# Joining small TensorE products into fewer visits in a hybrid mLSTM and attention decoder step

## The chip, the cores and the metric

The kernel runs on one core of a Trainium2 chip. The metric is the device time of one execution in microseconds; lower is better. The engines are called as in the profile: PE (TensorE, matrix products), DVE (VectorE), ACT (ScalarE), POOL (GpSimd), SP (SyncE, which issues most DMAs).

## What is computed

One layer of a decoder is applied to a prompt of 1024 tokens and to 8 samples of 4 tokens each (32 rows), with a width of 1024. Two branches run in parallel: an mLSTM with 4 heads of 128, in chunks of 128 tokens for the prompt, and sliding-window attention with 8 heads and 2 key-value heads. Both are gated and added back to the input. Cut to what matters here:

```python
h, gate = adaln_in(x, c, w_ada, b_ada, g_norm)
(mq, mk, mv, mi, mf, mo, mz, aq, ak, av, az, gm, ga) = split_in(h @ w_in)
y_m, C, n, m = mlstm_branch(mq, mk, mv, mi, mf, mo, mz, C0, n0, m0, b_i, b_f, g_mn)
...                                       # y_a: window attention, gated by silu(az)
u = sigmoid(gm) * (y_m @ w_mo) + sigmoid(ga) * (y_a @ w_ao)
x = x + gate * (u @ w_o)

# mlstm_chunk, per head: the samples' chunk has 4 tokens and starts from a given state C, n, m
num = einsum('bhts,bhse->bhte', s, v) + w_inter[..., None] * einsum('bhtd,bhde->bhte', q, C)
dot = sum(s, -1) + w_inter * einsum('bhtd,bhd->bht', q, n)
h = num / maximum(abs(dot), exp(-m_hat))[..., None]
...
# mlstm_branch, behind all chunks
h = h * rsqrt(mean(h * h, -1, keepdims=True) + NORM_EPS)
h = h * g_mn * sigmoid(mo) * silu(mz)
```

## The kernel before

All weights and activations are float32. A large product is made of three products in float32r (high part by high, high by low, low by high), 128 weights wide, with 288 to 512 columns; these are called long products here. From about a quarter of the time on they come in pairs of weight columns (`block_products`, class `Pair`): seven block products numbered 1 to 7 stand for eight, on 512 tokens at a time, into the banks `bx`, `bw`, `by` and `bz`. There are 18 such pairs: 4 of the mLSTM's inputs (`head_in`), 8 of gates (`gate`), 2 of `query_gate` and 4 of `head_gate`. Four further pairs for the attention's output (`AttPair`, `att_products`, banks `ax` to `az`) follow, then plain products by `w_mo` and by `w_o`.

Everything else on PE is small float32 products put between the long ones. PE's order is written out by the program: `mm` and `tr` append each product behind the last one (`in_order`). Class `Side` decides where small work goes. It holds generators in streams (`m` the prompt's heads, `a` the attention units, `s` the samples, `x` and `g` preparations). After each triple of long products `side.tick()` looks for generators that are due. Its clock `side.now` is a sum of estimated product times. A generator yields a lag and the PSUM banks its next step needs (`a`, `b`, `o`); a step that needs banks goes only at a visit, which comes at the earliest 1.5 us of that clock after the last one, and each bank is held back for a while after it was used (`HOLD`). Every tag of PSUM has two buffers, taken in turn.

The small products that the change touches, by the names that the profile shows:

- `smp`: the 32 sample rows against the raw weights of a pair, sixteen products of 32 columns each, spread over four column groups of the array (`Pair.samples`); its sum is copied to `smps`.
- `smpo`: one product that adds the four parts of `smps` (`samples_end`); its result goes to the pair's kind (`kind.samples`). In `block_products` it stands behind block product 6, while the next pair's `smp` stands behind product 2 (product 7 for the first pair).
- `ty`: transposition of the prompt head's eight normalised blocks (`head`, `stage_d`), three visits of 3, 3 and 2, each a step after the scaling of its blocks on DVE (`stage_c3`).
- `stk`, `sS`, `sn`, `sU`, `st`, `sty`: the steps of a sample head (`sample_head`), one of four: transposed keys and values, scores, numerator, state update (`sU`, two visits of 2 and 1), the sum over four partition groups (`st`), and the transposition of the normalised result (`sty`). Between `st` and `sty` stand a square sum on ACT and a chain of small DVE operations (`factors`) on 32 rows.
- `pt`, `oT`, `sc`: attention units; `tk`, `tv`, `S`, `U`, `n`: steps of the prompt's heads; they are not changed but lie beside the others.

On-chip memory: most tiles come from the tag `half` (128 x 512 float32), 49 buffers taken in turn. An unused tile `lead` of 56 values stands near the front of the allocation.

Of the kernel before, what the change touches and what calls it, by code (L numbers as in the profile page):

```python
# [37 lines left out]
C_END = 849  # L38
LEAD = 56

# [73 lines left out]
class Side:  # L114
# [25 lines left out]

    def tick(self):
        self.each()
        for st in self.streams.values():
            if st["wait"] and len(st["live"]) < st["max"] and self.now >= st["next"]:
                self.begin(st)
        used, visit = set(), self.now >= self.last + self.quiet
        for item in sorted((i for st in self.streams.values() for i in st["live"]), key=lambda i: i[1]):
            banks = set(item[2])
            if self.now < item[1] or used & banks or (banks and not visit) or any(self.now < self.free.get(b, 0) for b in banks):
                continue  # L150
            used |= banks
# [23 lines left out]
def body(tc, a):  # L175
    nc = tc.nc
    with ExitStack() as ctx:
# [17 lines left out]
        def ht(shape, name, dt=F32):  # L195
            return sp.tile(shape, dt, tag="half", bufs=49, name=name)

# [110 lines left out]
        load_x(1, 0, KT, xT[1])  # L308
        cp.tile([128, LEAD], F32, name="lead")
        cst = cp.tile([128, C_END], F32, name="cst")  # L310
# [287 lines left out]
        def gates(gp, zg, bias):  # L598
            gate_sums(gp, zg, (8,))
            ig = cp.tile([128, 36], F32, name="ig")  # L600
            x = cp.tile([128, 36], F32, name="fx")
            for t, o in ((ig, 0), (x, 4)):
# [4 lines left out]
                V.tensor_tensor(t[:NS, 32:36], gp[:NS, 8, o:o + 4], bias[:NS, o:o + 4], op=ALU.add)  # L607
            e = cp.tile([128, 36], F32, name="fe")
            S.activation(e, x, AF.Abs)
            S.activation(e, e, AF.Exp, scale=-1.0)  # L610
            r = cp.tile([128, 36], F32, name="fr")
            q = cp.tile([128, 36], F32, name="fq")
            lf = cp.tile([128, 36], F32, name="lf")
# [25 lines left out]
            gt4 = ht([32, 4, 128], "gt4")  # L639
            gt2 = ht([32, 2, 128], "gt2")  # L640
            aT, bT, zero, cm = (gt4[:, i] for i in range(4))
            nm, wi = gt2[:, 0], gt2[:, 1]
            aTs = cp.tile([NH, NS], F32, name="aTs")
# [387 lines left out]
        def head(h):  # L1031
# [100 lines left out]
            def stage_d(p):  # L1132
                cs = GROUPS[p]
                m = len(cs)
                c0, w = cs[0] * 128, m * 128
                ns = w_.pop(p)
                ty = pb([128, 3, 128], f"ty{h}_{p}")
                for i in range(m):
                    tr(ty[:, i], ns[:, i, 0:128], ident)
                y = ht([128, 384], "yt")[:, :w]  # L1140
                S.activation(y, ty[:, :m].rearrange("p c e -> p (c e)"), AF.Copy, scale=gmn[:, h:h + 1])
                issue(yhD[h][:, c0:c0 + w], y, eng=nc.gpsimd)

            for visit in ([(load, 0), 11.0, ""], [(prep, 0), 3.0, "ob"], [(stage_e, 0), (stage_a, 0), 7.0, "o"],
# [3 lines left out]
                          [(stage_e, 2), (stage_c, 1), (stage_a, 2), 7.0, "o"], [(stage_b, 2), 5.0, "o"],  # L1148
                          [(stage_c, 2), 5.0, ""], [(stage_f, 0), 4.0, ""], [(stage_c3, 0), 4.0, "b"],
                          [(stage_d, 0), (stage_c3, 1), 4.0, "b"], [(stage_d, 1), (stage_c3, 2), 4.0, "b"], [(stage_d, 2), 0.0, ""]):  # L1150
                for fn, p in visit[:-2]:
# [5 lines left out]
            if h == 2:  # L1157
                at["n0"], at["n1"] = (cp.tile([128, NH, NB], F32, name=n) for n in ("n0", "n1"))
                dma(at["n0"], a["state_n"])
                for i in range(NH):  # L1160
                    side.add("s", sample_head(i), "ob")

        def sample_head(h):
# [53 lines left out]
            for c, b, m in zip(Cs, bs, ns_):  # L1217
                V.tensor_tensor(c[:, :m], c[:, :m], sxb[:, h, 2, b].unsqueeze(2).to_broadcast((128, m, 129)), op=ALU.mult)
            yield 4.0, "b"
            for i, (c, b, m) in enumerate(zip(Cs, bs, ns_)):  # L1220
                up = pb([128, 388], f"sU{h}_{i}")
                mm(up[:, :m * 129 + m % 2], kn, vms[i][1][:, :m * 129 + m % 2], start=True, stop=True)
                V.tensor_tensor(c[:, :m], c[:, :m], up[:, :m * 129].rearrange("p (b e) -> p b e", e=129), op=ALU.add)
                store(a["C_s"][h][:, b], c[:, :m, 0:128])
                G.tensor_copy(at["n1"][:, h, b], c[:, :m, 128])
                if i == 1:
                    yield 1.5, "b"
            yield 3.0, "o"
            tot = po([128, 129], f"st{h}")
            mm(tot[:NS], cst[:, C_S32:C_S32 + NS], ns4, start=True, stop=True)  # L1230
            ns = sm([NS, 129], "sns", 1)
            S.copy(ns, tot[:NS])
            ssq = sm([NS, 1], "sssq", 2)
            jk = sm([128, 128], "mjk", 2, BF16)
            S.activation(jk[:NS], ns[:, 0:128], AF.Square, accum_out=ssq)
            yield 2.5, ""
            den = sm([NS, 1], "fsden", 2)
            size(den, ns[:, 128:129])
            d, r = factors(den, fls[:, h:h + 1], ssq, [NS, 1], "fs")
            yield 4.0, ""  # L1240
            V.tensor_scalar(ns[:, 0:128], ns[:, 0:128], d, r, op0=ALU.mult, op1=ALU.mult)
            yield 4.0, "b"
            ty = pb([128, NS], f"sty{h}")
            tr(ty, ns[:, 0:128], ident[:NS, :NS])
            V.tensor_scalar(gs[:, h], ty, gmn[:, h:h + 1], None, op0=ALU.mult)
            samples_done.append(h)
            if h == NH - 1:
# [247 lines left out]
        def block_products(jobs, hook):  # L1495
# [178 lines left out]
        def att_products():  # L1674
# [26 lines left out]
            for j, (n, i) in enumerate(flat):  # L1701
# [647 lines left out]
```

## Time and profile before

| | |
|---|---|
| time, median of 3 runs | 835.4 us (835.07 to 835.62) |
| the profiled execution's own time | 835.73 us |
| its span from first to last instruction | 833.9 us |
| PE busy | 813.9 us (98%) |
| DVE busy | 597.2 us (72%) |
| ACT busy | 421.7 us (51%) |
| granted TensorE clock | 0.999 |
| bytes moved | 153.95 MB, mean 185 GB/s |

How to read it: busy time is the union of an engine's instructions. PE's rows overlap, since a product starts while the one before it drains, so the cost of a product is seen in the distance between starts, not in its duration. A row of the timeline has the start and the duration in us, the engine, the line, the operation, the tile written and the tiles read, the shape (the first pair is rows by columns of the array) and a count; a small float32 product stands as two rows, a transposition as one. A row of PE's waits has who waited, for whom, us in total, times, longest. A window's row has for each engine the busy time and the count, then the granted clock, the busy share of the DMA engines and GB/s.

### The profile page before, as it was taken

Reading aid. Unit: us, or ns where it says so; the run is one execution under the profiler, and the core shown is the slowest. Engines: PE = TensorE matmul, PEld = TensorE weight load, DVE = VectorE, ACT = ScalarE, POOL = GpSimd, SP = SyncE. Lnnn points to the kernel's source line nnn. Section 1 sums busy time; section 2 is a strip of 40 time slices with the busy share of each in tenths; the row PEclk is TensorE's granted clock in tenths of the full one; section 3 lists DMA queues with packets and bytes.
Section 4 is the critical chain, followed back from the end, with each engine's and each line's share of the span. In section 5 each row is a group of like instructions: output and inputs, shape, how many; then the busy total and the mean of one; then the engine's idle time right before and its main releaser. Section 6 shows DMA issues by size and latency. Waiting matters only on the chain. (4 is left out here: it accounts for less than half of the span.)

```text
span 833.9 us, 15075 instructions
## 1 busy us (share of the span) xinstructions
PE 813.9 (98%) x5129; PEld 665.7 (80%) x5129; DVE 597.2 (72%) x1501; ACT 421.7 (51%) x1032; POOL 67.0 (8%) x128
## 2 busy tenths in 40 slices
PE   6999999999999999999999999999999999999996
PEld 3779897888787788888888877778777779997775
DVE  4899886656656455666666776787878988874776
ACT  5664365655565564535464545344445654334343
POOL 0120000000000000000000100000002104250000
PEclk9999999999999999999999999999999999999999
DMA  9996756346445423589845433554346685643532
GB/s 342 387 362 216 197 191 203 118 155 212 140 136 162 113 102 107 172 258 309 267 146 191 134 132 113 167 178 128 128 153 205 200 287 185 205 139 127 202 108 107
DMA packets 106688, 153.95 MB, mean 185 GB/s; under 512 B 20448, under 2 KB 54368, under 8 KB 106580
## 3 DMA queue, kind: packets, MB, share of 16 engines
q1 hardware_dynamic: 100964, 142.25, 52.3%
q10 hardware_dynamic: 4176, 6.56, 2.1%
q0 software_dynamic: 1472, 4.20, 1.3%
q8 instruction: 40, 0.66, 0.3%
q14 instruction: 36, 0.29, 0.1%
HBM read 109.22 MB, written 44.75 MB: 185 GB/s over the span
## 5 line engine op out<-in xcount | busy, mean ns | idle before, releaser
L221 ACT ACTIVATE p<-p,nmx 128x256 f32<-128x256 f32 (+1 forms) x64 | 31.0, 485 | 15.6 <-DVE nmx L221 15.2
L260 PE MATMUL g_aq<-h_h,wh_aq 128*128 128x384 f32 (+1 forms) x96 | 32.3, 336 | 0.0
L221 DVE CUSTOM_DVE_ANT_0 p<-sc,cst,sink 128x256 f32<-128x256 f32 (+1 forms) x64 | 26.2, 463 | 8.3 <-PE sc L260 8.2
L260 PE MATMUL g_aq<-h_h,wl_aq 128*128 128x384 f32 (+1 forms) x96 | 30.9, 322 | 0.0
L260 PE MATMUL g_aq<-h_l,wh_aq 128*128 128x384 f32 (+1 forms) x96 | 30.8, 321 | 0.0
L260 PE MATMUL g_w_mo<-ym_l,wh_w_mo 128*128 128x384 f32 (+1 forms) x96 | 30.8, 321 | 0.0
L260 PE MATMUL g_w_mo<-ym_h,wh_w_mo 128*128 128x384 f32 (+1 forms) x96 | 30.8, 321 | 0.0
L260 PE MATMUL g_w_mo<-ym_l,wl_w_mo 128*128 128x384 f32 (+1 forms) x96 | 30.8, 321 | 0.0
L248 POOL DMA_DIRECT2D oD<-uqv x16 | 8.9, 554 | 200.0 <-ACT uqv L221 162.8
L221 ACT ACTIVATE et<-et,an 128x128 f32<-128x128 f32 x32 | 11.2, 395 | 20.7 <-DVE et L221 19.2
L260 PEld LDWEIGHTS g_aq<-h_h,wh_aq 128*128 128x128 f32 x96 | 18.0, 188 | 2.6 <-issue 1.5
L260 PE MATMUL sc<-ukv,uqv 64*128 64x256 f32 (+1 forms) x128 | 18.3, 390 | 1.3 <-DVE p L221 1.2
L221 DVE COPY p<-pt 128x512 f32<-128x512 f32 (+1 forms) x16 | 10.5, 655 | 12.0 <-PE pt L265 12.0
L260 PEld LDWEIGHTS g_w_mo<-ym_l,wh_w_mo 128*128 128x128 f32 x96 | 18.0, 188 | 0.0
L260 PEld LDWEIGHTS g_aq<-h_l,wh_aq 128*128 128x128 f32 x96 | 18.0, 188 | 0.0
L260 PEld LDWEIGHTS g_w_mo<-ym_h,wh_w_mo 128*128 128x128 f32 x96 | 18.0, 188 | 0.0
L260 PEld LDWEIGHTS g_w_mo<-ym_l,wl_w_mo 128*128 128x128 f32 x96 | 18.0, 188 | 0.0
L260 PEld LDWEIGHTS g_aq<-h_h,wl_aq 128*128 128x128 f32 x96 | 18.0, 188 | 0.0
L221 ACT ACTIVATE p<-p,den 128x256 f32<-128x256 f32 (+1 forms) x32 | 14.2, 490 | 7.4 <-DVE den L221 7.3
L221 ACT ACTIVATE sq<-rows_h 128x512 f32<-128x512 f32 (+2 forms) x14 | 8.2, 582 | 17.7 <-issue 12.0
L260 PE MATMUL g_mq<-h_h,wh_mq 128*128 128x384 f32 (+1 forms) x48 | 16.8, 350 | 0.3 <-ACT mk L221 0.3
L221 DVE TENSOR_TENSOR wor<-wor,gb 128x512 f32<-128x512 f32 x16 | 10.7, 689 | 8.7 <-DMA wor<-w_out 8.6
(2078 smaller groups left out, 2852.1 us busy)
## 6 DMA issues: line engine op xcount, KB each, us to landing
x<-xT SPq DMA_DIRECT2D x16, 256.0 KB, 5.1
early_h<-w_ada SPq DMA_DIRECT2D x8, 512.0 KB, 8.8
adar_ga<-w_ada SPq DMA_DIRECT2D x16, 256.0 KB, 4.2
wr_ga<-w SPq DMA_DIRECT2D x16, 256.0 KB, 3.4
wr_gm<-w SPq DMA_DIRECT2D x16, 256.0 KB, 3.3
taD<-gt SPq DMA_DIRECT2D x16, 256.0 KB, 2.0
tmD<-gt SPq DMA_DIRECT2D x16, 256.0 KB, 4.2
wor<-w_out SPq DMA_DIRECT2D x16, 256.0 KB, 5.3
```

The costliest lines, as they stand in the source:

```text
L221: ins = f(*args, **kw)
L248: ins = (eng or nc.sync).dma_start(out, in_)
L260: in_order(nc.tensor.matmul(out, lhsT, rhs, start=start, stop=stop, skip_group_check=more))
```

## The change

- `samples_end` of a pair moves to directly ahead of `samples` of the next pair (the last pair's goes ahead of its product 3), in `block_products` and in `att_products`.
- Right after `samples`, `block_products` forces a visit (`side.tick(True)`), with bank `b` marked as just used.
- The prompt head scales all its blocks in one step and transposes all eight in one visit; the third block's tile comes from `o`.
- A sample head makes its three state updates in one visit, the third in a bank of `o`. Heads 0 and 2 end there; heads 1 and 3 carry on for both: one visit of two `st`, one chain of factors on two columns, one visit of two `sty`.
- Room: temporaries of the gates move into a `half` tile, `sns` into the head's own tile, `lead` goes, `half` gets a 50th buffer.

```diff
-LEAD = 56
...
-    def tick(self):
+    def tick(self, visit=False):
...
-        used, visit = set(), self.now >= self.last + self.quiet
+        used, visit = set(), visit or self.now >= self.last + self.quiet
...
-            return sp.tile(shape, dt, tag="half", bufs=49, name=name)
+            return sp.tile(shape, dt, tag="half", bufs=50, name=name)
...
-        cp.tile([128, LEAD], F32, name="lead")
...
-            x = cp.tile([128, 36], F32, name="fx")
+            gt2 = ht([128, 512], "gt2")
+            x, e, r, q = (gt2[:, 256 + 36 * i:292 + 36 * i] for i in range(4))
...
-                ty = pb([128, 3, 128], f"ty{h}_{p}")
+                ty = (pb, pb, po)[p]([128, 3, 128], f"ty{h}_{p}")
...
-                          [(stage_c, 2), 5.0, ""], [(stage_f, 0), 4.0, ""], [(stage_c3, 0), 4.0, "b"],
-                          [(stage_d, 0), (stage_c3, 1), 4.0, "b"], [(stage_d, 1), (stage_c3, 2), 4.0, "b"], [(stage_d, 2), 0.0, ""]):
+                          [(stage_c, 2), 5.0, ""], [(stage_f, 0), 4.0, ""], [(stage_c3, 0), (stage_c3, 1), (stage_c3, 2), 6.0, "ob"],
+                          [(stage_d, 0), (stage_d, 1), (stage_d, 2), 0.0, ""]):
...
-            yield 4.0, "b"
+            yield 4.0, "ob"
             for i, (c, b, m) in enumerate(zip(Cs, bs, ns_)):
-                up = pb([128, 388], f"sU{h}_{i}")
+                up = (pb, pb, po)[i]([128, 388], f"sU{h}_{i}")
...
-                if i == 1:
-                    yield 1.5, "b"
+            tails.append((h, ns4))
+            if h % 2 == 0:
+                return
             yield 3.0, "o"
-            tot = po([128, 129], f"st{h}")
-            mm(tot[:NS], cst[:, C_S32:C_S32 + NS], ns4, start=True, stop=True)
-            ns = sm([NS, 129], "sns", 1)
+            tot = po([128, 2, 129], f"st{h}")
+            for i, (_, n4) in enumerate(tails):
+                mm(tot[:NS, i], cst[:, C_S32:C_S32 + NS], n4, start=True, stop=True)
+            ns = z[:NS, 0:258].rearrange("p (m e) -> p m e", e=129)
...
-            d, r = factors(den, fls[:, h:h + 1], ssq, [NS, 1], "fs")
+            d, r = factors(den, fls[:, h - 1:h + 1], ssq, [NS, 2], "fs")
...
-            ty = pb([128, NS], f"sty{h}")
-            tr(ty, ns[:, 0:128], ident[:NS, :NS])
-            V.tensor_scalar(gs[:, h], ty, gmn[:, h:h + 1], None, op0=ALU.mult)
-            samples_done.append(h)
+            ty = pb([128, 2, NS], f"sty{h}")
+            for i, (g, _) in enumerate(tails):
+                tr(ty[:, i], ns[:, i, 0:128], ident[:NS, :NS])
+                V.tensor_scalar(gs[:, g], ty[:, i], gmn[:, g:g + 1], None, op0=ALU.mult)
+                samples_done.append(g)
+            tails.clear()
...
+                if i == 3 and not nxt:
+                    job_.samples_end()
...
                 if i == 6:
                     Y = filled(pa, "by", W, n)
-                    job_.samples_end()
...
                 if i == (2 if n else 7) and nxt:
+                    job_.samples_end()
                     nxt.samples()
+                    side.free["b"] = side.now + HOLD["b"]
+                    side.tick(True)
                     nxt.first_sums()
...
                     Y = copy_of(pa, "ay", W)
-                    job_.samples_end()
+                    if not nxt:
+                        job_.samples_end()
                 elif i == 2:
                     job_.done(0, 0, X)
                     if nxt:
+                        job_.samples_end()
                         nxt.samples()
                         nxt.first_sums()
```

More of the change, by code (lines that the diff above doesn't have):

```diff
@@ L607, in gates @@
                 V.tensor_tensor(t[:NS, 32:36], gp[:NS, 8, o:o + 4], bias[:NS, o:o + 4], op=ALU.add)
-            e = cp.tile([128, 36], F32, name="fe")
             S.activation(e, x, AF.Abs)
             S.activation(e, e, AF.Exp, scale=-1.0)
-            r = cp.tile([128, 36], F32, name="fr")
-            q = cp.tile([128, 36], F32, name="fq")
             lf = cp.tile([128, 36], F32, name="lf")
@@ L639, in gates @@
             gt4 = ht([32, 4, 128], "gt4")
-            gt2 = ht([32, 2, 128], "gt2")
             aT, bT, zero, cm = (gt4[:, i] for i in range(4))
-            nm, wi = gt2[:, 0], gt2[:, 1]
+            nm, wi = gt2[:32, 0:128], gt2[:32, 128:256]
             aTs = cp.tile([NH, NS], F32, name="aTs")
@@ L1161, in head @@
                     side.add("s", sample_head(i), "ob")
+        tails = []
         def sample_head(h):
@@ L1225, in sample_head @@
                 G.tensor_copy(at["n1"][:, h, b], c[:, :m, 128])
-                if i == 1:
-                    yield 1.5, "b"
+            tails.append((h, ns4))
+            if h % 2 == 0:
+                return
             yield 3.0, "o"
-            tot = po([128, 129], f"st{h}")
-            mm(tot[:NS], cst[:, C_S32:C_S32 + NS], ns4, start=True, stop=True)
-            ns = sm([NS, 129], "sns", 1)
+            tot = po([128, 2, 129], f"st{h}")
+            for i, (_, n4) in enumerate(tails):
+                mm(tot[:NS, i], cst[:, C_S32:C_S32 + NS], n4, start=True, stop=True)
+            ns = z[:NS, 0:258].rearrange("p (m e) -> p m e", e=129)
             S.copy(ns, tot[:NS])
-            ssq = sm([NS, 1], "sssq", 2)
-            jk = sm([128, 128], "mjk", 2, BF16)
-            S.activation(jk[:NS], ns[:, 0:128], AF.Square, accum_out=ssq)
+            ssq = sm([NS, 2], "sssq", 2)
+            for i in range(2):
+                jk = sm([128, 128], "mjk", 2, BF16)
+                S.activation(jk[:NS], ns[:, i, 0:128], AF.Square, accum_out=ssq[:, i:i + 1])
             yield 2.5, ""
-            den = sm([NS, 1], "fsden", 2)
-            size(den, ns[:, 128:129])
-            d, r = factors(den, fls[:, h:h + 1], ssq, [NS, 1], "fs")
+            den = sm([NS, 2], "fsden", 2)
+            size(den, ns[:, :, 128])
+            d, r = factors(den, fls[:, h - 1:h + 1], ssq, [NS, 2], "fs")
             yield 4.0, ""
-            V.tensor_scalar(ns[:, 0:128], ns[:, 0:128], d, r, op0=ALU.mult, op1=ALU.mult)
+            for i in range(2):
+                V.tensor_scalar(ns[:, i, 0:128], ns[:, i, 0:128], d[:, i:i + 1], r[:, i:i + 1], op0=ALU.mult, op1=ALU.mult)
             yield 4.0, "b"
-            ty = pb([128, NS], f"sty{h}")
-            tr(ty, ns[:, 0:128], ident[:NS, :NS])
-            V.tensor_scalar(gs[:, h], ty, gmn[:, h:h + 1], None, op0=ALU.mult)
-            samples_done.append(h)
+            ty = pb([128, 2, NS], f"sty{h}")
[4 more added lines that the diff above has]
+            tails.clear()
             if h == NH - 1:
```

## The prediction

> **What bounds the kernel now.** I read the page's head first, then the waits of PE, then the stages by window, and last the timeline of PE around single small products.
>
> ```profile
> span 833.9 us, 15075 instructions
> PE 813.9 (98%) x5129; PEld 665.7 (80%) x5129; DVE 597.2 (72%) x1501; ACT 421.7 (51%) x1032; POOL 67.0 (8%) x128
> ```
>
> ```profile
> PE xc L260 <- ACT xsq L221: 7.1, 1, 7.1
> PE sc L260 <- DVE p L221: 1.2, 1, 1.2
> ```
>
> ```profile
> 0.00:60.00 60.00, 51.35 (x346) 36.07 (x350) 43.39 (x117) 37.16 (x61) 7.74 (x17) 1.00 0.99 368
> 60.00:834.00 774.00, 762.55 (x4787) 629.67 (x4779) 553.77 (x1385) 384.49 (x971) 59.30 (x111) 1.00 0.53 170
> ```
>
> PE is busy for 813.9 of 833.9 us and follows a written order. From 60 us on it idles for 11.4 us of 774 (762.55 busy). The largest wait of all is the 7.1 us before the first product, which this change does not touch; the next is 1.2 us. So the end is set by how long PE takes to walk its list. An edit counts if it shortens that list, puts a wait into it or takes one out. DVE (72%) and ACT (51%) count only where PE waits for them. The clock column is 1.00 in both windows, so nothing is to be had there.
>
> "Busy" does not say what one product costs, since rows overlap. I therefore price by start-to-start times: the last long product ahead of a small one, up to the second long product behind it, less two steps between long products.
>
> ```profile
> 493.07 0.39 PE L260 MATMUL bw<-h_l,wh_pgate__5807 128*128 128x512 f32 x1
> 493.30 0.39 PE L260 MATMUL bw<-h_h,wl_pgate__5808 128*128 128x512 f32 x1
> 493.62 0.41 PE L260 MATMUL st<-sz,cst 128*32 128x129 f32 x2
> 493.95 0.50 PE L260 MATMUL bw<-h_h,wh_pgate__5807 128*128 128x512 f32 x1
> 494.29 0.40 PE L260 MATMUL bw<-h_l,wh_pgate__5807 128*128 128x512 f32 x1
> ```
>
> A step between long products is 0.23 us (493.07 to 493.30). Around one `st` product (a float32 product stands as two rows) it is 493.30 to 494.29: 0.99, less 0.46, so one lone `st` costs 0.53 us. Its two flanks show where: 0.32 to get in instead of 0.23, and 0.34 for the first long product behind it instead of 0.23. About 0.20 us is thus the price of the visit, not of the product. This is what joining can win, if the partner has such flanks too.
>
> ```profile
> 503.32 0.39 PE L260 MATMUL bw<-t2h,wl_pgate__5900 128*128 128x512 f32 x1
> 503.55 0.33 PE L260 MATMUL smpo<-cst,smps 128*128 128x64 f32 x2
> 503.68 0.48 PE L260 MATMUL bx<-h_h,wh_pgate__5955 128*128 128x512 f32 x1
> 504.00 0.40 PE L260 MATMUL bx<-h_l,wh_pgate__5955 128*128 128x512 f32 x1
> ```
>
> A lone `smpo` costs 504.00 - 503.32 - 0.46 = 0.22 us. It is 128 columns wide and goes in without any flank (0.23), and its own step is 0.13. All small products are not alike, then: the 32-column ones (`128*32`) pay at both ends, the 128-column ones hardly at all.
>
> ```profile
> 483.66 0.39 PE L260 MATMUL bx<-h_h,wl_pgate__5676 128*128 128x512 f32 x1
> 483.98 0.30 PE L260 MATMUL smp<-wr_ga,c 128*32 128x128 f32 x2
> ...
> 484.77 0.28 PE L260 MATMUL smp<-wr_ga,c 128*32 128x128 f32 x2
> ...
> 485.32 0.40 PE L260 MATMUL by<-t3l,wh_pgate__5705 128*128 128x512 f32 x1
> ```
>
> The sixteen `smp` products cost 485.32 - 483.66 - 0.46 = 1.20 us alone, and they too are entered by a flank of 0.32; between 483.98 and 484.77 lie seven passes of 0.11 each.
>
> **The change part by part.** In the order in which the two programs are built, PE has the same number of products, long and small; the runs of small products between long ones fall from 160 to 127. So no product goes, only flanks.
>
> *`smpo` moved next to `smp`.* Of 22 `smpo`, 20 now stand directly beside an `smp` or `smpa` run (17 and 3); before, 21 stood alone and one stood ahead of an `oT` run, 64 columns wide:
>
> ```profile
> 273.25 0.39 PE L260 MATMUL bw<-t2h,wl_phead_in__3365 128*128 128x512 f32 x1
> 273.48 0.33 PE L260 MATMUL smpo<-cst,smps 128*128 128x64 f32 x2
> 273.74 0.44 PE L260 MATMUL oT<-p,ukv 128*64 128x128 f32 x4
> ```
>
> From the long product to `oT` it is 0.49. Apart they would take 0.22 for `smpo` and 0.32 for the way in (as `smp` shows): 0.54. The neighbour keeps its flank, and 0.05 us is won. Bounds per join: nothing, if the narrow run costs the same behind any product, and 0.20, both flanks. I take 0.05, as this row is the same product in the same place: 19 joins, 0.95 us.
>
> *`st` in pairs.*
>
> ```profile
> 574.84 0.39 PE L260 MATMUL bx<-h_h,wl_phead_gate__6697 128*128 128x512 f32 x1
> ...
> 576.06 0.38 PE L260 MATMUL st<-sz,cst 128*32 128x129 f32 x2
> ...
> 576.71 0.40 PE L260 MATMUL by<-t3l,wh_phead_gate__6726 128*128 128x512 f32 x1
> ```
>
> Here an `st` already follows an `smp` run: 1.87 - 0.46 - 1.20 = 0.21 us for it, 0.32 less than alone. Before, three stood alone and this one was joined: 3 x 0.53 + 0.21 = 1.80. Now there are two runs of two. The second goes to the same columns as the first, so it costs two passes of 0.11, 0.22 (at most 0.53, if it waits for the first to drain): 2 x 0.75 = 1.50. Gain 0.30 us.
>
> *`sty` in pairs.*
>
> ```profile
> 588.52 0.39 PE L260 MATMUL bz<-h_h,wl_phead_gate__6868 128*128 128x512 f32 x1
> ...
> 589.35 0.39 PE L260 MATMUL bz<-h_l,wh_phead_gate__6867 128*128 128x512 f32 x1
> ```
>
> Between these two long products stand one `sty` and the first long product behind it. Alone it costs 0.83 - 0.46 = 0.37; one of four was behind an `smp` run, for which I take the 0.21 of `st`. The second of a pair lies between one pass (0.11) and 0.21; I take 0.16. Before 3 x 0.37 + 0.21 = 1.32, now 2 x 0.53 = 1.06: 0.26 us.
>
> *`sn` behind `smp`.* The forced visit right after the `smp` run lets two of the four `sn` runs follow it. Both are 32 columns wide. Bounds 0.05 (the `oT` row) and 0.32 (the `st` row); the `st` row is of the same width and also 129 columns long, so 0.32: 0.64 us for two.
>
> *The head's `ty` in one run of eight instead of 3 + 3 + 2, and `sU` in one of three.*
>
> ```profile
> 490.89 0.39 PE L260 MATMUL bx<-h_h,wl_pgate__5729 128*128 128x512 f32 x1
> 491.12 0.49 PE L265 MATMUL ty<-cst,et 128*128 128x128 f32 x3
> ...
> 491.69 0.39 PE L260 MATMUL bw<-h_l,wh_pgate__5807 128*128 128x512 f32 x1
> ```
>
> Three transpositions cost 0.80 - 0.46 = 0.34, 0.11 each, which is one pass: nothing is left for the visit. This part, the one with the most runs removed (eight of 33), I cost at nothing. `sU` is 128 columns wide like the long products and gets nothing either. A doubt of 0.05 per removed run, 12 runs, is up to 0.6 us more.
>
> *Off the path.* The sample heads' factors run twice instead of four times on DVE; with PE at 98% that frees DVE and moves no end. The scaling of the head's eight blocks (`stage_c3`) is now issued at once, 6 us ahead of the transpositions; DVE needs eight small operations for it, so the cover holds unless DVE is blocked for most of that time, in which case `ty`, and all of PE's list behind it, waits. `samples_end` stands right after the copies of `done(0, 0, X)` on ACT and DVE; what it adds there is the same work as at its old place. No DMA is added or taken away; only the times at which SP issues some of them move. `half` has 50 buffers instead of 49, and `lead` goes.
>
> **Sum:** 0.95 + 0.30 + 0.26 + 0.64 = 2.15 us. The profiled run took 835.73 us for a span of 833.9; less the sum it is 833.6. The median of the runs shown is 835.4, 0.3 lower, so I predict 833.2 us. With the joins at nothing and `st` and `sn` at their bad ends hardly anything is left; with 0.20 per join it is 5 us. Its own range is 831.6 to 834.6.
>
> I call 0.2% of the time, 1.67 us, about what a measurement of this kernel can tell from no change: faster means under 833.7, slower over 837.1.
>
> **The rivals.**
>
> *The flanks stay.* If the join with `smp` is worth nothing because every change of width costs its 0.09 to 0.11 us wherever it happens, the 0.95 goes; with `sn` at the `oT` row's 0.05, 0.54 more. Left is 0.66: 834.7 us, no change. For it speaks that `smpo` has almost no flank of its own; against it the 0.32 measured behind `smp`.
>
> *A bank not free takes the place of the flank.* `smpo` and `smp` now come back to back and take both buffers of bank `b`, so `smp` gets the one used last. The third `ty` and third `sU` take a bank of `o`, and once a run of scores (`sc`, both `o` buffers) is followed at once by `pt`, of which half goes to `o`.
>
> ```profile
> L221 DVE CUSTOM_DVE_ANT_0 p<-sc,cst,sink 128x256 f32<-128x256 f32 (+1 forms) x64 | 26.2, 463 | 8.3 <-PE sc L260 8.2
> ```
>
> That bank is free only after two reductions of 463 ns, 0.93 us, of which four transpositions (0.44) hide half: some 0.5 us once, more if DVE is held up, as in the 1.2 us wait quoted above. Over 20 joins a wait of 0.11 us each undoes the sum; 0.19 us each makes it slower by over 0.2%. At 0.15 us per join it is 3.0 us: 836.2. Against it: in the built order the last use of `b` ahead of a join is at least six long products (1.4 us) away, and often thirty.
>
> [...]
>
> [...]
>
> [...]
>
> **How the numbers follow.** The forecast gets 0.64: 0.56 of it under 833.7, 0.08 between that and 834.6. The flanks that stay get 0.14, all within 0.2%. The bank gets 0.14, half within 0.2%, half slower. The moved tiles get 0.08, slower. Faster 0.56, same 0.08 + 0.14 + 0.07 = 0.29, slower 0.15. The range from 831.4 to 836.6 holds the forecast, the flanks and the nearer part of the bank case, and leaves out the tiles.
>
> **What would show it.** Right: the way from the long product before a joined `smpo` to the second long product after `smp` is about 1.83 us, where apart they would add up to 0.22 + 1.66 = 1.88; a pair of `st` 1.21; an `sn` run behind `smp` 0.3 less than one that stands alone; eight `ty` 0.88. PE's waits after 60 us sum to about as much as before. Wrong: a new line in PE's waits with `smp`, `smpo`, `pt` or `ty` on it (the bank), or the first `g_ak` product later and the first 60 us with less moved per second (the tiles).

## The result, and the profile after

The changed kernel takes 838.4 us (median of 10 runs, 837.06 to 839.88) beside 835.3 us of the kernel before on the same chip (834.47 to 836.06). The ratio is 1.0035, with a 95% interval from 1.0026 to 1.0045: slower by about 3 us, where a gain of 2.15 us was forecast. The profiled run took 838.28 us for a span of 836.5, 2.6 us longer than the span before.

The head of the page after, the row of PE's clock in 40 slices, and two windows, the second of them also for the kernel before, in the last line (columns: PE, PEld, DVE, ACT and POOL busy, then granted clock, DMA share, GB/s):

```profile
span 836.5 us, 15032 instructions
PE 812.5 (97%) x5129; PEld 670.9 (80%) x5129; DVE 595.0 (71%) x1479; ACT 420.1 (50%) x1030; POOL 67.4 (8%) x128
PEclk9999999999999999999899999999999999999998
60.00:836.50 776.50, 760.44 (x4788) 635.08 (x4779) 551.65 (x1365) 382.91 (x969) 59.88 (x111) 0.99 0.53 171
340.00:465.00 125.00, 119.54 (x716) 100.92 (x715) 79.19 (x181) 61.59 (x160) 4.66 (x19) 0.97 0.62 208
...
340.00:465.00 125.00, 124.63 (x772) 103.81 (x771) 80.47 (x179) 65.07 (x164) 4.37 (x13) 1.00 0.70 227
```

From 60 us to its end PE was busy for 762.55 of 773.9 us before, and idle for 11.35. Now it is busy for 760.44 of 776.5 and idle for 16.06. So the list got 2.11 us shorter, and the idle time 4.71 us longer: together the 2.60 us of the span. The new idle time lies in one stretch, 340 to 465 us, where 5.5 us are idle (125 less 119.54) that were 0.4 before (124.63 busy): 5.1 us more there, and a little less elsewhere. The clock in this stretch is 0.97 on the mean.

PE's waits after:

```profile
PE S L259 <- DVE C L220: 5.5, 1, 5.5
PE pt L264 <- DVE mx L220: 1.1, 1, 1.1
PE sty L264 <- DVE gs L220: 1.1, 2, 0.8
```

These three lines (source and operation, the one waited for, then us in total, times, longest) follow the wait ahead of the first product, which is 6.4 us now and was 7.1. They are new or grown: `S` waited for `C` 0.4 us before, once. The timeline of PE and DVE at that place:

```profile
405.16 0.38 PE L264 MATMUL tv<-cst,hv 128*128 128x128 f32 x2
411.00 1.22 PE L259 MATMUL S<-hq,hk 128*128 128x128 f32 x4 [5.46 <-DVE C L220]
411.87 0.77 PE L259 MATMUL bw<-t2h,wh_pgate__4792 128*128 128x512 f32 x1
412.45 0.63 PE L259 MATMUL bw<-t2l,wh_pgate__4792 128*128 128x512 f32 x1
...
415.01 0.63 PE L259 MATMUL bx<-h_l,wh_pgate__4824 128*128 128x512 f32 x1
415.43 0.52 PE L259 MATMUL bx<-h_h,wl_pgate__4825 128*128 128x512 f32 x1
...
402.50 0.35 DVE L220 SCALAR_TENSOR_TENSOR C<-C,dec,U 128x129 f32<-128x129 f32 x1
...
409.50 0.56 DVE L220 TENSOR_TENSOR et<-et,cst 128x384 f32<-128x384 f32 x1 [6.06 <-DMA et<-nmd]
...
410.60 0.34 DVE L220 SCALAR_TENSOR_TENSOR C<-C,dec,U 128x129 f32<-128x129 f32 x1
...
403.51 0.42 SPq L247 DMA_DIRECT2D et<-nmd  x1
```

Read from the bottom. SP issues the load of `et` at 403.51; DVE's add on it can begin at 409.50, 6.0 us later. DVE is idle for 6.06 us until then, and the third step of the state `C` of head 3 comes behind the add (402.50 is the second step, 410.60 the third). Until that step has read `U`, its `o` buffer is not free, and the `S` run of head 2, which needs it, stands still on PE from 405.5 to 411.0. Behind it PE goes at half speed (granted clock 0.50 from 411 to 414 us): from 411.87 to 415.43 lie eight steps of 0.445 on the mean instead of 0.228, 1.7 us more.

The same place in the kernel before: the load is late there too (`et` is issued at 414.95 and its add begins at 418.78, 3.8 us later, where it is 6.0 now), but the third `C` stands ahead of the add.

```profile
415.91 0.71 PE L260 MATMUL S<-hq,hk 128*128 128x128 f32 x4 [0.37 <-DVE C L221]
...
415.51 0.34 DVE L221 SCALAR_TENSOR_TENSOR C<-C,dec,U 128x129 f32<-128x129 f32 x1
...
418.78 0.56 DVE L221 TENSOR_TENSOR et<-et,cst 128x384 f32<-128x384 f32 x1 [1.05 <-DMA et<-nmd]
```

What the prediction priced is there as priced in these places:

```profile
490.32 0.39 PE L259 MATMUL bx<-h_h,wl_pgate__5730 128*128 128x512 f32 x1
490.55 0.33 PE L259 MATMUL smpo<-cst,smps 128*128 128x64 f32 x2
...
492.15 0.39 PE L259 MATMUL by<-t3l,wh_pgate__5791 128*128 128x512 f32 x1
...
509.24 0.39 PE L259 MATMUL bw<-t2h,wl_pgate__5971 128*128 128x512 f32 x1
509.56 0.63 PE L259 MATMUL st<-sz,cst 128*32 128x129 f32 x4
...
510.46 0.39 PE L259 MATMUL bw<-t2l,wh_pgate__5970 128*128 128x512 f32 x1
```

`smpo` with `smp` takes 1.83 (492.15 - 490.32), a pair of `st` 1.22 (510.46 - 509.24), both with the two long steps that the prediction takes off elsewhere. Eight `ty`, read in the same way, take 0.88 without those steps.

### The profile page after: what moved, and what is told of

Read it like the earlier page. It is cut to its first block, busy times and chain, and to the rows that moved or that the text cites. A ratio compares the mean times of both kernels' runs of the same rounds, so it can differ in the third digit from the quotient of the medians.

```text
span 836.5 us, 15032 instructions
## 1 busy us (share of the span) xinstructions
PE 812.5 (97%) x5129; PEld 670.9 (80%) x5129; DVE 595.0 (71%) x1479; ACT 420.1 (50%) x1030; POOL 67.4 (8%) x128
## 4 chain that ended last, share of the span: by engine, by line
PE 91%; DVE 4%; DMA 2%; ACT 1%; issue 1%; SPq 1%; DVEq 0%; ACTq 0%
PE bx L259 11%; PE bw L259 11%; PE by L259 11%; PE g_aq L259 6%; PE bz L259 6%; PE g_w_mo L259 5%; PE g_mq L259 3%; PE foW L259 3%; PE foX L259 3%; PE foY L259 2%; PE smp L259 2%; PE oT L259 2%; PE foZ L259 2%; PE sc L259 2%; PE pt L264 2%; PE g_ak L259 1%
## 5 line engine op out<-in xcount | busy, mean ns | idle before, releaser
L220 DVE TENSOR_TENSOR et<-et,cst 128x384 f32<-128x384 f32 (+1 forms) x12 | 6.1, 512 | 16.5 <-DMA et<-nmd 16.5
L264 PE MATMUL pt<-cst,p 128*128 128x128 f32 x120 | 16.4, 277 | 1.1 <-DVE mx L220 1.1
```

The lines of the kernel that those rows point to most:

```text
L220: ins = f(*args, **kw)
L264: in_order(nc.tensor.transpose(out, in_, idn))
```

## The experiments

The first theory was this: the joined runs are worth what was summed, and one wait with its half clock eats it. The rivals: the moved tiles, or the joins themselves. Each ratio below is to the kernel before on the same chip.

**Four single edits.** They are cut to the lines that matter:

```diff
 # c_first: both DVE operations of prep are ordered behind the last C of the block before
+for ins in (V.tensor_tensor(et[:, :m], et[:, :m], cmask.unsqueeze(1).to_broadcast((128, m, 128)), op=ALU.add),
+            V.tensor_tensor(qw[:, :m], qw[:, :m], q[:, :m * 128].rearrange("p (c e) -> p c e", e=128), op=ALU.mult)):
+    if "c" in w_:
+        no_sync(getattr(ins, "ins", ins), [w_["c"]])
+w_["c"] = getattr(ins, "ins", ins)          # in stage_b, behind its last C
 # sty: both transpositions first, then DVE's reads
-for i, (g, _) in enumerate(tails):
+for i in range(2):
     tr(ty[:, i], ns[:, i, 0:128], ident[:NS, :NS])
+for i, (g, _) in enumerate(tails):
     V.tensor_scalar(gs[:, g], ty[:, i], gmn[:, g:g + 1], None, op0=ALU.mult)
 # no lead (in the kernel before)
-cp.tile([128, LEAD], F32, name="lead")
 # ty alone (in the kernel before)
-ty = pb([128, 3, 128], f"ty{h}_{p}")
+ty = (pb, pb, po)[p]([128, 3, 128], f"ty{h}_{p}")
-[(stage_c3, 0), 4.0, "b"], [(stage_d, 0), (stage_c3, 1), 4.0, "b"], [(stage_d, 1), (stage_c3, 2), 4.0, "b"], [(stage_d, 2), 0.0, ""]
+[(stage_c3, 0), (stage_c3, 1), (stage_c3, 2), 6.0, "ob"], [(stage_d, 0), (stage_d, 1), (stage_d, 2), 0.0, ""]
```

The order alone, in the changed kernel:

> The changed kernel with one order set on DVE: the two operations of a prompt head's prep, which wait for loads, may not stand ahead of the last C of the block before. PE's order is the same. Theory A (one wait on DVE): S loses the 5.5 us wait on C but for some 0.4, and the 8 long products at half clock behind it (0.20 us each) with the slow S run go too, 7 us in all: 831.3 us, granted clock 0.999. Theory B (the moved tiles make the transfers land later): the load still lands late, the wait shows up at another product of that head, and the time stays over 836.

Measured: 836.1 us, 0.9991 [0.9978, 1.0003], not the 831.3 of theory A. The wait of `S` is gone, but two of 1.6 and 1.4 us took its place, and the clock is still low there: the slice of the page from 396 to 417 us reads 8 tenths, as that from 397 to 418 us does in the changed kernel (9 before):

```profile
PE smpo L259 <- ACT hv L220: 1.6, 1, 1.6
PE smp L259 <- ACT hk L220: 1.4, 1, 1.4
```

The load is as late as it was (the add waits 4.72 us for it). ACT's exponentials of `et` wait for it too, and the copies of `tv` and `tk` that free the `b` buffers stand behind them: in the changed kernel ACT is idle for 7.56 us until the exponentials begin at 410.10, and the copies begin at 412.38 and 413.11. So DVE's order decides how much is lost, and the late load is what there is to lose. That the wait would show up at another product is what theory B said; its reason, the moved tiles, is not borne out, since the add waits as long (4.81 us) where the tiles have not moved (the `ty` part alone, below).

The order of `sty`, in the changed kernel:

> The changed kernel with both transpositions of a pair of sample heads ahead of the two reads by DVE. If the second transposition waits only because the first one's read stands between them (0.3 and 0.8 us), both waits go: 1.1 us less, 837.3 us. If DVE's reads were late for another reason, the wait moves to the next user of the bank and nothing is won: 838.4.

Measured: 837.1 us, 0.9997 [0.9986, 1.0008]. The waits of `sty` are gone from the profile and `S` still waits 5.3 us. The time is the one expected (837.3); by the ratios (1.0035 to 0.9997) it would be 3.2 us less, more than the two waits had. In this profile the clock also falls less: the slice of the page from 396 to 417 us reads 9 tenths, where that from 397 to 418 us reads 8 in the changed kernel, and the mean is 0.996 where it is 0.993; that lies over 100 us ahead of the first `sty`, and why is not shown.

The kernel before without `lead`:

> The kernel before without the unused tile lead, so that all tiles move by 224 bytes, and nothing else. Theory B (moved tiles): the loads of the first 60 us take longer and the time rises by 2 us or more, to 837.3 or over. Theory A (one wait on DVE): 835.3 within 0.5.

Measured: 837.0 us, 1.0006 [0.9994, 1.0017]. The tiles moved by 224 bytes cost nothing that can be measured, so that rival falls: it asked for 2 us or more. Of its two signs one is there: in the first 60 us 358 GB/s are moved, here and in the changed kernel, where it was 368. The first `g_ak` product begins 0.2 to 0.3 us later in both (25.14 before), but 0.2 us earlier in the run with the order alone, where the tiles have moved too.

The kernel before with the `ty` part alone:

> The kernel before with only the prompt head's part: one scaling step and one run of eight transpositions. By the price in the prediction a visit of ty costs nothing, so 835.3 within 0.6, the 0.6 being whatever the moved order does to single waits. If a visit did cost 0.2 us, eight fewer would give 833.7.

Measured: 841.3 us, 1.0056 [1.0043, 1.0069]. This is the part that the prediction costed at nothing. The timeline of PE and DVE has the same picture as the full change:

```profile
410.34 1.22 PE L260 MATMUL S<-hq,hk 128*128 128x128 f32 x4 [4.63 <-DVE C L221]
...
408.82 0.56 DVE L221 TENSOR_TENSOR et<-et,cst 128x384 f32<-128x384 f32 x1 [4.81 <-DMA et<-nmd]
...
409.94 0.34 DVE L221 SCALAR_TENSOR_TENSOR C<-C,dec,U 128x129 f32<-128x129 f32 x1
```

With eight visits fewer, what follows in the list has moved, and the C that came ahead of the add comes behind it. The joins of `smpo`, `st` and `sn` are not needed for the wait; whether they would bring it about without the `ty` part was not run, nor were the three things in this part (one scaling step, one visit, the third bank) tried apart. The full change stands at 1.0035 and this part at 1.0056. The difference, 0.0021 or 1.8 us, is near the 2.15 us of the sum, but it can be put down to the rest of the change only if both kernels lose the same by their waits, and they don't quite (`S` 5.5 us and 4.6).

**The loads from another queue.** Next to settle was why the load is late. It stands on SP behind the stores of `wor` and `gt`, which wait for DVE and ACT.

```diff
-dma(t[:, :w], d[:, c0:c0 + w])                    # hq, hk, hv; et and qw alike
+stores(d.tensor); issue(t[:, :w], d[:, c0:c0 + w], eng=nc.gpsimd)
```

> The changed kernel with one edit: the five loads of a prompt head's group (hq, hk, hv, et, qw) are issued from GpSimd's queue and not from SyncE's, where they stood behind a store that waits for DVE (woDb, 396.39, 3.19 us). DVE's order still has et's add ahead of head 3's third C. Theory A (the load stands in SyncE's queue, DVE's add waits for it, the third C behind the add keeps the o buffer that S needs, and the long idle of PE halves the clock): et lands before its add, PE's wait S<-DVE C of 5.5 us falls under 1 us, the 8 or 9 steps of 0.43 us behind it go too; of 838.4 us some 7.4 go: about 831 us, ratio 0.993 to 0.996. Rival B (the load is late because its buffers come free late or the transfer itself is slow): the wait stays above 3 us and the ratio is 1.000 or more. Rival C (GpSimd's queue delays them too, or the stores of yt behind them): a wait on hq, hk or hv in PE, ratio 0.998 to 1.002.

Measured: 845.9 us, 1.0116 [1.0095, 1.0136]: worse by far. The timeline says why. This is the issue of a load in POOL's queue with what it waited for, and the wait of PE that came of it:

```profile
416.27 0.55 POOL L247 DMA_DIRECT2D qw<-wid  x1 [6.64 <-DMA taD<-gt]
...
421.80 1.22 PE L259 MATMUL S<-hq,hk 128*128 128x128 f32 x4 [7.65 <-DVE C L220]
```

The buffer of `qw` held a `gt` tile whose store was only under way; `hv` waited in the same way 2.5 us at 407.8. On POOL's queue these two loads waited for those stores, 6.6 and 2.5 us. Theory A was wrong in its cure, and rival B was right here.

The `ty` part alone, with these loads:

> The kernel before with only the ty part of the change (one run of eight transpositions, third ty in a bank of o), as in the run that gave 1.0056, and the head's five loads issued from GpSimd's queue. Theory A: the wait of 4.6 us and the half clock behind it (about 2 us) go, 841.3 less 6.5 is about 835, ratio 0.996 to 1.000: the ty part by itself is worth about nothing. Rival D (the merged run costs time by itself, since DVE's eight scalings at once and the third bank delay other work): ratio 1.002 or more though the wait for C is gone.

Measured: 849.6 us, 1.0155 [1.0135, 1.0174], with a wait of `S` for `C` of 8.5 us. It decides nothing on `ty` itself, since the wait did not go.

The changed kernel with these loads and both orders:

> The changed kernel with three edits: the head's loads from GpSimd's queue, both transpositions of a sample pair ahead of DVE's reads of them (the waits of sty, 1.1 us in all, go), and prep's two DVE operations held behind the last C of the block before. Theory A: as with the loads alone, less 1 us: about 830 us, ratio 0.992 to 0.995, PE's waits after 60 us sum to under 4 us. Rival B: the loads land late all the same, and PE waits for smp or smpo behind ACT's copies as in the run with the order alone: ratio 0.998 to 1.000.

Measured: 842.0 us, 1.0063 [1.0048, 1.0079]. Both theories were off: `S` waits for `C` twice, 5.7 us in all. At the longer wait (4.7 us) the add on `et` now stands behind the third `C` (414.89), but another operation on a late load, of `w_out`, stands ahead of it on DVE:

```profile
414.28 0.69 DVE L220 TENSOR_TENSOR wor<-wor,gb 128x512 f32<-128x512 f32 x1 [5.61 <-DMA wor<-w_out]
```

The changed kernel with these loads and single sample heads:

> The changed kernel with the head's loads from GpSimd's queue, and the sample heads ended one at a time as before (st, sty alone, sU in two visits, no third bank for sU); smpo, sn and ty stay joined. By the prediction's prices the pairs are worth 0.30 us (st) and 0.26 us (sty); against that stand the waits of the paired sty of 1.1 us. So beside the paired kernel with the same loads: slower by 0.5 us if the prices alone count, faster by 0.5 us if the waits count too, in both cases within 0.15%. A difference above 0.3% would say that the pairing moves something else, with a wait in PE's list that has st, sty, sU or smp on it.

Measured: 848.0 us, 1.0132 [1.0110, 1.0154], against 1.0116 for the paired kernel with the same loads: not to be told apart.

**Taking the stores out of SP's queue instead.**

```diff
...                            # store() takes an engine
-store(woD[name, k], t)
+store(woD[name, k], t, nc.gpsimd)
```

> The changed kernel with one edit: the stores of the output weights (woDp, woDb), each of which waits for DVE's wor, are issued from GpSimd's queue; the head's loads stay on SyncE's, and the orders of PE and DVE are those of the changed kernel. Theory A3 (the loads are late because SyncE's queue stands at woDb<-wor, 396.39 for 3.2 us, ahead of them): hq is issued about 3 us earlier, et lands as much earlier, the wait S<-DVE C of 5.5 us falls to about 2.5, the idle of PE is then too short for the half clock: 838.4 less 3 and 2 is 833.4, ratio 0.996 to 0.999. Rival B2 (the loads wait for their buffers, not for the queue): hq is issued within 1 us of where it was, the wait is 4.5 us or more, ratio 1.002 to 1.004.

Measured: 841.0 us, 1.0050 [1.0033, 1.0066]. `S` waits 5.6 us, as rival B2 had it, and `bw` waits 2.0 us for DVE's `ws`, which is new. SP's queue, the add and PE there:

```profile
404.37 0.32 SPq L247 DMA_DIRECT2D taD<-gt  x1
...
405.94 0.42 SPq L247 DMA_DIRECT2D hq<-qD  x1
...
407.39 0.42 SPq L247 DMA_DIRECT2D et<-nmd  x1
...
414.20 0.56 DVE L220 TENSOR_TENSOR et<-et,cst 128x384 f32<-128x384 f32 x1 [6.91 <-DMA et<-nmd]
```

Without `woDb` ahead of them the loads stand behind the next store, `taD<-gt`. `hq` is issued 4.3 us ahead of the last `tv` (410.24) instead of 3.1 (402.08 to 405.16): 1.2 us won, not 3, and given back, since the add comes 6.8 us after the issue instead of 6.0. So the queue's stand at `woDb` is not the cause. That an idle of some 2.5 us is too short for the half clock, as theory A3 had it, was the author's estimate, and the runs show both: in this one the 2.0 us that `bw` waits are followed by a clock of 0.60 and 0.55 (406 to 408 and 408 to 410 us), with the pause alone (below) 2.7 us by one of 1.00.

> The same stores from GpSimd's queue, with prep's two DVE operations behind the last C of the block before and both transpositions of a sample pair ahead of DVE's reads; the pause stays 10. Theory A3: no wait of S, smpo or smp over 0.7 us near 405, sty's waits gone: about 831 us, ratio 0.993 to 0.996. Rival B2: smpo and smp wait for ACT about 3 us as in the run with the order alone: 0.998 to 1.000.

Measured: 836.0 us, 0.9992 [0.9978, 1.0006]: as the order alone and as rival B2 forecast, with `smpo` behind ACT's `hv` 2.1 us and `smp` behind `hk` 1.4 (and `bw` behind DVE's `ws` 1.4). The load is late in both runs (the add waits 6.91 us for `et` and 5.23), whichever stores stand ahead of it.

**More time between load and use.**

```diff
-[(stage_b, 0), (load, 1), 10.0, ""]
+[(stage_b, 0), (load, 1), 14.0, ""]      # and the same for (load, 2)
```

With that pause, the order (c_first) and the order of `sty`, in the changed kernel:

> The changed kernel with three edits: the pause between a prompt head's load of the next group and its prep is 14 us of product time instead of 10 (twice per head), prep's two DVE operations stand behind the last C of the block before, and both transpositions of a sample pair stand ahead of DVE's reads. The loads stay on SyncE's queue. Theory A2 (after the run with GpSimd's queue: the load is late because its buffers are those of gt tiles that are only being stored, so it needs time, not another queue): PE's waits S<-DVE C (5.5) and, as in the run with the order alone, smpo and smp behind ACT (3.0) are both under 1 us, no row of steps of 0.43 us after 60 us, 838.4 less 5.5, 2.0 and 1.1 is about 830: ratio 0.992 to 0.995. Rival E (a later prep moves the wait to another place, for instance to the last head's end or to the sample heads behind it): a new wait of 2 us or more in PE's list, ratio 0.997 to 1.003.

Measured: 833.2 us, 0.9977 [0.9968, 0.9987]: faster than both kernels. The span is 830.7 and PE's waits after the first are:

```profile
PE by L259 <- DVE gt L220: 2.0, 2, 1.7
...
PE bw L259 <- ACT bw L220: 0.7, 1, 0.7
PE pt L264 <- DVE mx L220: 0.6, 1, 0.6
60.00:830.70 770.70, 759.74 (x4787) 632.75 (x4779) 549.87 (x1365) 382.63 (x969) 58.68 (x111) 1.00 0.53 172
```

No `S`, no `sty`, a clock of 1.00. The last line is the window from 60 us: busy 759.74, idle 10.96, where before it was 762.55 and 11.35. With the idle time as before, the span is 3.2 us shorter and 2.8 of that is PE's shorter list. These are two single executions; by the ratio of the runs the gain is 1.9 us. The waits that theory A2 named are gone, but its ratio (0.992 to 0.995) was not reached: 0.9977 lies in the range of rival E, whose new wait is there too (`by` waits 2.0 us for DVE's `gt`).

The pause alone, in the changed kernel:

> The changed kernel with the longer pause (14) alone, of the three edits that together gave 0.9977. Theory G (the pause moves the two head loads of this stretch ahead of woDb in SyncE's queue, 385 to 390, so et is there in time): no wait S<-DVE C over 1 us, sty's 1.1 us still there: ratio 0.998 to 1.000. Rival H (DVE's order is what the gain came from): a wait for C of 3 us or more, ratio over 1.002.

Measured: 838.6 us, 1.0028 [1.0013, 1.0043]. The same wait is there, later and shorter: head 3's first `C` begins at 414.43 (402.17 in the changed kernel), and head 2's `S` waits 2.7 us from 418 on for the third one (420.57), which stands behind the add (420.10) that waits 4.4 us for `et`. Theory G was wrong, and rival H nearly right (its ratio is met, the wait is 2.7 us and not 3). Beside the kernel before, the pause without the order is no gain, and the order without the pause none that can be told from zero (0.9991); together, and with the order of `sty`, 0.9977.

The kernel before with the pause and the order:

> The kernel before with the longer pause (14) and the same order of prep behind C. It has no wait of this kind to lose: S 0.4 us and sc 1.2 us. Theory A2: 0 to 1.5 us faster, ratio 0.998 to 1.000; then what the changed kernel has with the same two edits is the change's own worth, some 2.2 us by the prediction's sum, 1.1 of it less where a wait of pt stays. Rival F (the longer pause is what gains, whatever the change): ratio as in the changed kernel with it, 0.992 to 0.995.

Measured: 843.4 us, 1.0096 [1.0082, 1.0109]. I expected no harm, and had it wrong. `pt` waits 1.9 us, with a mean clock of 0.98 from 232 to 340 us (1.00 in the best version), and the longest wait is further on. PE's longest wait after the first product, and DVE's row:

```profile
PE smpo L260 <- ACT hv L221: 4.9, 1, 4.9
...
409.86 0.43 DVE L221 TENSOR_TENSOR et<-et,cst 128x256 f32<-128x256 f32 x1 [4.90 <-DMA et<-nmd]
```

The kernel before has the same trap. Its own order and pause happen to step around it, which is luck, since nothing in the program sets that order; with these two edits it falls in, through ACT this time. With only the `ty` part in it as well:

> The kernel before with only the ty part of the change (1.0056 by itself), the longer pause and the order of prep behind C. Theory A2: the ty part is worth nothing once the loads are in time, so the same as the kernel before with these two edits, within 0.15%: ratio 0.997 to 1.001, no wait S<-DVE C over 1 us. Rival D (the merged run costs by itself): 0.3% or more above it.

Measured: 843.5 us, 1.0101 [1.0087, 1.0115], within 0.05% of the one before, as that expectation said (beside it, not in its absolute numbers). But its wait is another: `tv` waits 6.5 us for ACT's copy to `smps`, and ACT stood there 3.7 us for a store (`taD<-gt`), not for a load. Two different waits came out alike, so this says nothing of what the part costs by itself.

The best version with the sample heads ended one at a time (and without the order of `sty`, which then does not arise):

> The changed kernel with the longer pause and the order, and the sample heads ended one at a time (st and sty alone, sU in two visits). Beside the paired kernel with the same two edits: 0.56 us slower by the prediction's prices of the pairs (0.30 st, 0.26 sty), so ratio higher by 0.0007; if the pairing costs something (a longer wait before the heads' end), lower. A difference over 0.3% either way would come with a wait of st, sty, sU or smp in PE's list.

Measured: 833.8 us, 0.9982 [0.9972, 0.9993] beside 0.9977: 0.4 us slower where 0.56 was expected, less than these runs can tell apart. It is no clean price of the pairs either: in this trace two of the four `st` and one of the `sn` stand behind an `smp` run, which they don't in the version it is compared with.

The best version with both `pt` tiles in the banks of `b`:

> The version with the three edits (0.9977) and one more: both tiles of transposed scores (pt) lie in the banks of b, so that a run of scores that takes both buffers of o is not followed by a pt that needs one of them. If that wait (0.6 us at 289) is the bank's, it goes: 0.6 us less, ratio 0.9970. If another wait takes its place (the second pt then waits for the first one's reader, 16 times), PE's waits with pt on them grow by more than 1 us and the ratio is 0.999 or more.

Measured: 835.2 us, 0.9990 [0.9976, 1.0004]. The wait of `pt` is gone from the list, and a larger one came, as the second case had it but in another place (the transpositions of a head that follow a `pt` in `b`):

```profile
PE by L259 <- DVE gt L220: 3.9, 2, 2.1
PE tv L264 <- DVE p L220: 2.1, 1, 2.1
```

What stays open: what makes the transfer itself take 6 us there. The `half` buffers come free late (6.6 and 2.5 us on POOL's queue), and the DMA engines are busy while it lands (a share of 0.87 from 405 to 408 us in the changed kernel, 0.97 from 408 to 411), but the two were not parted.

## Why the prediction was wrong

**What held.** The prices by start-to-start times. `smpo` with `smp` 1.83, as forecast; a pair of `st` 1.22 (1.21); eight `ty` 0.88 (0.88); and the run of `smpo`, `smp` and `sn` takes 2.61 where it is 1.83 without `sn`, 0.78 more, while an `sn` run alone costs 1.11 (1.57 less 0.46): 0.33 won each (0.32). PE's busy time from 60 us on fell by 2.11 us in the changed kernel, in spite of the half clock in it, and by 2.8 in the best version.

**The step that failed** is the paragraph on `ty` and `sU`, the part with the most runs removed, which "I cost at nothing", and with it "the cover holds unless DVE is blocked". The sum had no term for a new wait, and the forecast took PE's waits to stay as they were; its idle time grew by 4.7 us. I asked whether DVE has time for the eight scalings ahead of `ty`. It has: no wait carries `ty`. I did not ask what the eight visits' absence does to the order of the rest of DVE's work. The `ty` part alone stands at 1.0056 (some 4.7 us), with a wait of 4.6 us at `S` and a mean clock of 0.993, as low as in the changed kernel. I had compared PE's order in both programs as built, and not DVE's, where the add on a late load stands ahead of a step that PE needs. The trace of before shows the other half, in DVE's waits:

```profile
DVE et L221 <- DMA et<-nmd: 12.0, 5, 5.0
```

Five times DVE stood still for `et`, up to 5.0 us, and PE's list of waits has nothing of that size. At 418.78 it was the order that kept the wait from PE; for the other four that is not shown.

**Mis-sized terms.** The pair of `sty`: the second was put at 0.16 us beyond the first, 0.53 for the pair. It took 1.17 on the mean (1.63 less 0.46), since DVE's read of the first one's half of the tile stands between the two transpositions. The first pair:

```profile
522.65 0.24 PE L264 MATMUL sty<-cst,sz 32*128 32x32 f32 x1
523.23 0.24 PE L264 MATMUL sty<-cst,sz 32*128 32x32 f32 x1 [0.34 <-DVE gs L220]
```

With both transpositions first, in the best version, it is 0.43 (0.89 less 0.46). The bank rival named the right place, `pt` behind `sc`, and put it at some 0.5 us; it took 1.1 in the changed kernel and 0.6 in the best version:

```profile
289.20 0.66 PE L264 MATMUL pt<-cst,p 128*128 128x128 f32 x4
290.97 0.66 PE L264 MATMUL pt<-cst,p 128*128 128x128 f32 x4 [1.11 <-DVE mx L220]
```

Its other half, a wait at each `smpo` join, did not come. No run shows that the place of the tiles, which got 0.08, costs time: moved alone, they gave 1.0006, and 358 GB/s in the first 60 us where it was 368.

**The account.** Of waits, 5.5 + 1.1 + 1.1 came, less 1.2 (`sc`), 0.8 (`bx`), 0.5 (`aw`), 0.4 (`S`), 0.3 (`smpo`) and 0.2 (`by`) that were there before: 4.3 of the 4.7 us by which PE's idle time grew. The half clock took 1.7 us of what the joins had won. The prediction's own list of signs named `smp`, `smpo`, `pt` and `ty` as the places of a new wait; `S` was not on it.

**Was the sum right, then?** In the best version the measured gain is 1.9 us by the ratio (0.0023 of 835.4), and the sum was 2.15. That is no proof, and that the two are close is partly luck: the version has three more edits, and the kernel before with two of them is slower. Besides, in its trace all four `sn` runs stand alone again (1.57 to 1.58 us each), so 0.64 of the sum is not in it, and `by` waits 2.0 us that it did not before. Yet its list is 2.8 us shorter, where the other terms make 1.51. The changed kernel says the same: with the half clock's 1.7 us taken off, its busy time fell by some 3.8 us (an estimate, 2.11 + 1.7) and not by 2.15. So the sum was too low for the list as well; where the rest comes from stays open. What the runs show is that the shorter list is there and that one wait decides whether anybody sees it.

## What to carry to other kernels

Where one engine is busy 98% of the time, a change to its list can change the order of the others' work too, as it did here. Compare the built order of each engine that feeds it, and look there for an operation on a late load that has come to stand ahead of one that frees a buffer. Joining a narrow visit won 0.05 to 0.33 us here; a single wait behind a load cost 5.5 us, with 1.7 us of half clock on top: secure the loads first, then count flanks.

## What was new of the hardware

The long product's step is 0.228 us at full clock (22 steps from 403.10 to 408.12 in the best version, clock 1.00), and 0.427 at the half clock that followed PE's idle of 5.46 us (six steps from 412.87 to 415.43 in the changed kernel). Granted clock by windows of 3 us in the changed kernel:

```profile
405.00:408.00 3.00, 0.54 (x5) 0.30 (x3) 0.00 (x0) 0.00 (x0) 0.00 (x0) 1.00 0.87 203
408.00:411.00 3.00, 0.00 (x1) 0.00 (x1) 1.44 (x4) 0.90 (x4) 0.00 (x0) 0.65 0.97 337
411.00:414.00 3.00, 3.00 (x9) 2.61 (x10) 2.27 (x5) 2.97 (x13) 0.10 (x1) 0.50 0.69 227
414.00:417.00 3.00, 3.00 (x11) 2.37 (x11) 1.39 (x3) 0.76 (x2) 0.00 (x0) 0.72 0.50 182
```

Shorter idles went with a lower clock in some places and not in others. In the version with `pt` in `b`, PE was idle for 1.85 us at one go, ran for some 1.3 us at full speed, and from 426.27 on made seven steps of 0.427 (granted clock 1.00 from 424 to 426 us, 0.53 from 426 to 428):

```profile
424.70 0.50 PE L259 MATMUL by<-t4h,wh_pgate__4966 128*128 128x512 f32 x1 [1.85 <-DVE gt L220]
...
426.27 0.63 PE L259 MATMUL by<-t4h,wh_pgate__4966 128*128 128x512 f32 x1
```

With the output weights' stores on POOL's queue a wait of 2.0 us was followed by a clock of 0.60 and 0.55. With the pause alone an idle of 2.7 us at 418 was followed by 1.00 in each window of 2 us up to 428. So in these runs the clock fell behind idles of 1.85 and 2.0 us and not behind one of 2.7, and the seven slow steps began 1.57 us after the wait was over; what decides it is not shown.
